# Where tokens and weight halves lie in SBUF: a 16-byte shift moved from one operand of the matmuls to the other

## The chip, the cores and the metric

The kernel runs on one core of a Trainium2 chip. The metric is the time of one execution in device microseconds: 1579.43 us is the median of three runs (1579.37 to 1579.49). One more execution was profiled; its trace is what is read below.

## The reference

One layer of an encoder on 256 tokens of width 4096, float32. What is computed:

```python
h = layer_norm(x, emb_ln_g, emb_ln_b)
p = h @ w_in                                   # 4096 x 13312: b, c, h, z of the convolution, q, k, v, z of attention
y_conv = c_b * centred_short_conv(c_c * c_h, conv_w) * silu(c_z)
y_attn = banded_window_attention(a_q, a_k, a_v, sink) * silu(a_z)   # 16 heads, 4 of keys and values, window 128
y = concatenate([y_conv, y_attn]) @ w_out      # 4096 x 4096
out = layer_norm(2 ** 0.25 * h + y, ln_g, ln_b)
```

## The kernel before

Both projections are made in a split form of float32: each operand is cut into a high half that TensorE's fp32r format holds exactly and a low half, what is left, and a product is three matmuls, high x high, high x low and low x high. The tokens are turned so that their 4096 features lie on the partitions; `xT` holds for each of 32 feature tiles 256 high and 256 low columns (1024 + 1024 bytes a partition). A slice of 128 token columns is the stationary operand of a matmul, loaded by a LDWEIGHTS of its own, and 256 columns of a weight half are the moving operand that streams past it.

The weights come from HBM in pieces of 128 x 2048 (`PIECE`) into the buffers `w0` to `w2` (and `w6` to `w8`, or free parts of `R`, where there is room). For each piece ScalarE writes the high half (`split_hi`, L201, into the tile `whi`), VectorE subtracts it for the low half (`split_lo`, L205, into `wlo`); both are rings of three tiles in the pool `wpool`. A plain piece is a step of 48 matmuls (`mm` with lines L253 to L255 for the input projection, `mm_out` with L920 to L922 for the output projection). A pair step (`mm_pair`, L277 to L279) multiplies two by two blocks with seven products in place of eight, 21 matmuls of the same shape; its stationary operands are slices of `xT` and sums of such slices that were made once: `SC` and `SC2` for the input stage (pool `psc`), `SCy` for the output stage, in the same memory as `SC`.

The order of instructions is written out by hand: a main loop over the steps issues, for step j, its matmuls, the high half for step j + 3, what is due of the attention or the convolution (transposes through `ident`, scores, exponentials, and so on), the loads of raw pieces up to seven steps ahead, and the low half for step j + 3. SP issues nearly all transfers. In the output stage `open_p2` closes the pools of the input stage and opens `p2`, with the result `R`, the parameter rows `gb` and others.

Two things of the kernel before bear on the change. The helper `shifted` makes a tile longer by 2 x `OFF` = 8 elements and hands out a view that begins 4 elements, 16 bytes, into it; `xT`, `SC` and `SC2` are made by it, `SCy`, `whi` and `wlo` are not. And small tiles named `gap` and `gap2` hold unused memory so that what follows lies where it does.

Of the kernel before, what the change touches and what calls it, by code (L numbers as in the profile page):

```python
# [8 lines left out]
F32 = mybir.dt.float32  # L9
F32R = mybir.dt.float32r  # L10
# [4 lines left out]
P = 128  # L15
D = 4096
S = 256
KT = D // P
# [9 lines left out]
PIECE = HK * P  # L28
# [4 lines left out]
W = 512  # L33
# [8 lines left out]
HT = S // 2  # L42
NP = 7
# [4 lines left out]
OP = 4  # L48
OUT_ORDERS = ["s" * 8] * 2 + ["sSsSsSsSss"] * 5 + ["", ""]
N_W = 3  # L50
OFF = 4


def units(ci):
# [45 lines left out]
def encoder_kernel(ctx: ExitStack, tc: tile.TileContext, x, emb_g, emb_b, wi, ws, conv_w, sink, wo, ln_g, ln_b, out):  # L100
# [3 lines left out]
    const = ctx.enter_context(tc.tile_pool(name="const", bufs=1))  # L104
    wpool = ctx.enter_context(tc.tile_pool(name="wpool", bufs=3))
    small = ctx.enter_context(tc.tile_pool(name="small", bufs=4))
# [9 lines left out]
    steps = IN_STEPS + OUT_STEPS  # L116
# [73 lines left out]
        return t[:, HW:] if is_pair(j) else t[:, 0:4 * HW] if steps[j][0] == "half" else t  # L190

    def half_tile(j, name):
        if j < len(steps) - 1:
            return wpool.tile([P, PIECE], F32R, name=name)
        (_, k), bs = w_bufs(j)
        user[bs[k]] = j
        return bs[k][0].tile([P, PIECE], F32R, name=bs[k][1], bufs=1)
# [20 lines left out]
    cw = const.tile([P, CONV_T, 3], F32, name="cw")  # L218
    sk = const.tile([P, HEADS], F32, name="sk")

    def shifted(pool, shape, name, **kw):

        n = math.prod(shape)
        t = pool.tile([P, n + 2 * OFF], F32R, name=name, **kw)[:, OFF:OFF + n]
        names = "abcd"[:len(shape)]
        return t.rearrange(f"p ({' '.join(names)}) -> p {' '.join(names)}", **dict(zip(names[1:], shape[1:])))

    xT = shifted(const, (KT, 2 * S), "xT")
    musd = const.tile([P, 2, 4], F32, name="musd")
    eps_t = const.tile([P, 1], F32, name="eps_t")  # L230
    nc.vector.memset(eps_t, LN_EPS)
    const.tile([P, 8], F32, name="gap")
    small.tile([P, 24], F32, name="gap2", bufs=1)


    acc = {}
# [56 lines left out]
    with tc.tile_pool(name="pro", bufs=1) as pro:  # L293
# [12 lines left out]
            sl = slice(h * PIECE // 2, (h + 1) * PIECE // 2)  # L306
            nc.sync.dma_start(out=first[1][:, sl], in_=wi[IN_PIECES.index(steps[1][1:])][:, sl])

        first = [wpool.tile([P, PIECE], F32, name=f"first{j}", tag="whi") for j in range(2)]
        x_load(0, 0, 1024, 2048, 3072, 3584, 3840, 4096)  # L310
        nc.sync.dma_start(out=g_c, in_=emb_g)
        nc.sync.dma_start(out=b_c, in_=emb_b)
# [146 lines left out]
    n_pro = 7  # L459


    ph, phs = ExitStack(), ExitStack()
    psc = ctx.enter_context(tc.tile_pool(name="psc", bufs=1))
    sc_tiles = [shifted(psc, (n, 2, 3, HT), name) for n, name in ((NP - 2, "SC"), (2, "SC2"))]
    SC = [sc_tiles[p // (NP - 2)][:, p % (NP - 2), :, :, :] for p in range(NP)]
    pw = phs.enter_context(tc.tile_pool(name="pw", bufs=1))
    extra.append((pw, "w6"))
# [98 lines left out]
    def s_add(h):  # L566
        slope = 2.0 ** (-8.0 * (h + 1) / HEADS)
        s = pa.tile([P, 2, S], F32, name="s")
        nc.vector.scalar_tensor_tensor(s, tab, slope, st_.pop(("s", h)), op0=ALU.mult, op1=ALU.add)
        m = small.tile([P, 2], F32, name="m")  # L570
        nc.vector.tensor_reduce(m, s, axis=AX.X, op=ALU.max)
        nm = small.tile([P, 2], F32, name="nm")
        nc.vector.tensor_scalar(nm, m, sk[:, h:h + 1], -1.0, op0=ALU.max, op1=ALU.mult)
        st_["sm", h] = s, nm

    def exps(h):
        s, nm = st_.pop(("sm", h))
        p = pa.tile([P, 2, S], F32, name="p", bufs=2)
        den = small.tile([P, 2], F32, name="den")
        es = small.tile([P, 2], F32, name="es")  # L580
        for b in range(2):
            nc.scalar.activation(p[:, b, :], s[:, b, :], AF.Exp, bias=nm[:, b:b + 1], accum_out=den[:, b:b + 1])
        nc.scalar.activation(es, nm, AF.Exp, bias=sk[:, h:h + 1])
        st_["p", h] = p, den, es
# [256 lines left out]
    def open_p2():  # L841
        nonlocal p2, R, st2, ms2, rows, t5, lhs5
        ph.close()
        phs.close()
        p2 = ctx.enter_context(tc.tile_pool(name="p2", bufs=1))
        R = p2.tile([P, 2, D], F32, name="R")
        st2 = [p2.tile([P, ncs, 6], F32, name=f"s2{i}") for i in range(2)]
        ms2 = p2.tile([P, 2, 4], F32, name="ms2")
        rows = p2.tile([P, 3 * W], F32R, name="rows")
        t5 = p2.tile([P, 2, 3, 32], F32, name="t5")  # L850
        nc.vector.memset(t5, 0.0)
        nc.vector.memset(t5[:, :, :, 3:5], 1.0)
        lhs5 = p2.tile([P, 2, P], F32R, name="lhs5")
# [18 lines left out]
    def res_load(n):  # L872
# [3 lines left out]
        if n < ncs - 1:  # L876
            gb = p2.tile([P, 3, w], F32, name="gb")
        if n < ncs - 2:
            xc = psc.tile([P, 2, w], F32, name="xc", tag="SC2")
        elif n == ncs - 2:  # L880
            zt.append(psc.tile([P, 8 * W], F32, name="z", tag="SC"))
            xc = zt[0][:, 6 * W:6 * W + 2 * w].rearrange("p (a b) -> p a b", a=2)
        else:
            z = zt[0]
            gb = z[:, 0:3 * w].rearrange("p (a b) -> p a b", a=3)
            xc = z[:, 3 * w:5 * w].rearrange("p (a b) -> p a b", a=2)
            g1, b1, t1 = (z[:, 5 * w + k * W:5 * w + (k + 1) * W] for k in range(3))
            first_cols.extend((g1, b1, t1, z[:, 5 * w + 3 * W:5 * w + 3 * W + P]))
            nc.sync.dma_start(out=g1, in_=bcast(ln_g, 0, W))
            nc.sync.dma_start(out=b1, in_=bcast(ln_b, 0, W))  # L890
# [109 lines left out]
    def y_sums(k):  # L1000
        nonlocal SC
        if k == 0:
            t = psc.tile([P, OP, 2, 4, HT], F32R, name="SCy", tag="SC")
            SC = [t[:, p, :, :, :] for p in range(OP)]
        x_sums(k, R[:, 0, 2 * W:4 * W])

# [126 lines left out]
```

## Time and profile before

| what | value |
|---|---|
| median of the runs | 1579.43 us |
| the profiled execution | 1580.26 us |
| its span, first to last instruction | 1578.5 us |
| granted TensorE clock | 0.999 |
| instructions | 29953, 12947 of them matmul entries on TensorE |
| moved by DMA | 316.17 MB, 200 GB/s on the mean |

In the rows below PE is TensorE's matmuls, PEld its weight loads, DVE VectorE, ACT ScalarE, POOL GpSimd, SP SyncE; L254 is line 254 of the kernel. A row that groups instructions has: line, engine, operation, tile written <- tiles read, shapes, xcount | busy us, mean ns of one | idle time of the engine before them, and what ended it. A matmul's duration in these rows is from its start until its modelled end, and successive matmuls overlap; how fast TensorE works through them is therefore seen from the distance of their starts, not from their durations. A row of one line's instructions gives the shortest, median and longest duration and, behind it, the start of the first and of the last in us; a row of the timeline begins with a start and a duration in us. A row on stretches gives the stretch, its length, the busy time of TensorE with the number of entries, the granted clock and the DMA share and rate. A row on waits says who waited <- for whom: us in all, times, longest.

### The profile page before, as it was taken

To read this page: it belongs to the slowest core of one execution; us is meant where nothing else is said; L and a number is where in the kernel's file an instruction comes from. 1 tells how busy PE (TensorE), PEld (TensorE's weight loads), DVE (VectorE), ACT (ScalarE), POOL (GpSimd) and SP (SyncE) were. 2 spreads that over 40 slices of the span, in tenths; PEclk is the share of its full clock that TensorE was granted. 3 is DMA by queue.
4 is the path that set the end of the run, shared out by engine and by line. 5 is a ranking of instruction groups with operands and counts; after the bars stand their busy time and mean duration, and the time that the engine had idled before them with its cause. 6 is when DMAs were issued, how large, how long until landed. Compare 5 with 4: busy or idle time off the path is not lost.

```text
span 1578.5 us, 29953 instructions
## 1 busy us (share of the span) xinstructions
PE 1564.9 (99%) x12947; PEld 1549.1 (98%) x12947; DVE 1331.6 (84%) x1555; ACT 780.0 (49%) x669; POOL 1.3 (0%) x7
## 2 busy tenths in 40 slices
PE   7999999999999999999999999999999999999998
PEld 4999999999999999999999999999999999999997
DVE  8669888889898898889898889888898688888866
ACT  5444546656565555544445445544455334443431
POOL 0000000000000000000000000000000000000000
PEclk9999999999999999999999999999999999999999
DMA  7545554555655555656555555556556656656563
GB/s 294 188 174 190 198 199 162 196 178 184 206 186 167 187 184 205 206 191 211 199 176 189 210 201 176 209 170 229 192 206 261 247 194 208 249 196 218 207 231 136
DMA packets 71748, 316.17 MB, mean 200 GB/s; under 512 B 8544, under 2 KB 12608, under 8 KB 50880
## 3 DMA queue, kind: packets, MB, share of 16 engines
q1 hardware_dynamic: 70608, 312.43, 57.0%
q8 instruction: 101, 1.65, 0.4%
q10 hardware_dynamic: 1008, 1.84, 0.3%
q14 instruction: 31, 0.25, 0.0%
HBM read 305.23 MB, written 8.91 MB: 199 GB/s over the span
## 4 chain that ended last, share of the span: by engine, by line
PE 98%; DVE 1%; DMA 0%; ACT 0%; issue 0%; SPq 0%; ACTq 0%
PE acc L254 15%; PE acc L253 15%; PE acc L255 15%; PE acc L920 7%; PE acc L921 7%; PE acc L922 7%; PE pacc L278 6%; PE pacc L279 6%; PE pacc L277 6%; PE acc L277 4%; PE acc L279 4%; PE acc L278 4%; PE att L492 1%; DVE st L330 0%; PE att L603 0%; PE acc L380 0%
## 5 line engine op out<-in xcount | busy, mean ns | idle before, releaser
L201 ACT ACTIVATE whi<-w 128x2048 fp32r<-128x2048 f32 (+1 forms) x354 | 620.7, 1753 | 674.6 <-PE acc L255 230.9
L205 DVE TENSOR_TENSOR wlo<-w,whi 128x2048 fp32r<-128x2048 f32 (+1 forms) x354 | 736.6, 2084 | 170.9 <-ACT whi L201 170.6
L253 PE MATMUL acc<-whi,xT 128*128 128x256 f32 x1976 | 562.7, 285 | 0.0
L254 PE MATMUL acc<-wlo,xT 128*128 128x256 f32 x1976 | 560.5, 284 | 0.0
L255 PE MATMUL acc<-whi,xT 128*128 128x256 f32 x1976 | 560.5, 284 | 0.0
L254 PEld LDWEIGHTS acc<-wlo,xT 128*128 128x128 f32 x1976 | 374.8, 190 | 0.1
L253 PEld LDWEIGHTS acc<-whi,xT 128*128 128x128 f32 x1976 | 374.9, 190 | 0.0
L255 PEld LDWEIGHTS acc<-whi,xT 128*128 128x128 f32 x1976 | 374.8, 190 | 0.0
L920 PE MATMUL acc<-whi,xT 128*128 128x256 f32 x848 | 241.4, 285 | 0.0
L922 PE MATMUL acc<-whi,xT 128*128 128x256 f32 x848 | 241.2, 284 | 0.0
L921 PE MATMUL acc<-wlo,xT 128*128 128x256 f32 x848 | 241.2, 284 | 0.0
L920 PEld LDWEIGHTS acc<-whi,xT 128*128 128x128 f32 x848 | 161.1, 190 | 0.4 <-issue 0.4
L921 PEld LDWEIGHTS acc<-wlo,xT 128*128 128x128 f32 x848 | 161.1, 190 | 0.0
L922 PEld LDWEIGHTS acc<-whi,xT 128*128 128x128 f32 x848 | 161.0, 190 | 0.0
L182 DVE TENSOR_TENSOR w<-w 128x512 f32<-128x512 f32 x179 | 122.3, 683 | 6.1 <-DMA w<-in_ws 6.1
L277 PE MATMUL acc<-whi,xT 128*128 128x256 f32 x370 | 105.0, 284 | 0.0
L279 PE MATMUL acc<-whi,xT 128*128 128x256 f32 x370 | 105.0, 284 | 0.0
L278 PE MATMUL acc<-wlo,xT 128*128 128x256 f32 x370 | 104.8, 283 | 0.0
L277 PE MATMUL pacc<-whi,xT 128*128 128x256 f32 x350 | 100.9, 288 | 0.0
L279 PE MATMUL pacc<-whi,xT 128*128 128x256 f32 x350 | 99.3, 284 | 0.0
L278 PE MATMUL pacc<-wlo,xT 128*128 128x256 f32 x350 | 99.3, 284 | 0.0
L278 PE MATMUL pacc<-wlo,SC 128*128 128x256 f32 x330 | 93.7, 284 | 0.0
(230 smaller groups left out, 2064.5 us busy)
## 6 DMA issues: line engine op xcount, KB each, us to landing
w<-in_wi SPq DMA_DIRECT2D x112, 1024.0 KB
w<-in_ws SPq DMA_DIRECT2D x202, 512.0 KB
w<-in_wo SPq DMA_DIRECT2D x41, 1024.0 KB
R<-in_wo SPq DMA_DIRECT2D x13, 1024.0 KB
x<-in_x SPq DMA_DIRECT2D x7, 512.0 KB
yl<-yd SPq DMA_DIRECT2D x7, 512.0 KB
xc<-in_x SPq DMA_DIRECT2D x14, 256.0 KB
R<-in_ws SPq DMA_DIRECT2D x6, 512.0 KB
```

Of the source, the lines that this page charges most:

```text
L182: nc.vector.tensor_tensor(s01, b22, b12.to_broadcast([P, 2, HW]), op=ALU.add)
L201: nc.scalar.activation(part(j, wh[j]), part(j, raw[j]), AF.Copy)
L205: nc.vector.tensor_tensor(part(j, wl[j]), part(j, raw[j]), part(j, wh[j]).bitcast(F32), op=ALU.subtract)
L253: nc.tensor.matmul(o, xh, hi[:, sl], start=(first and k == 0 and c == 0), stop=False)
L254: nc.tensor.matmul(o, xh, lo[:, sl], start=False, stop=False)
L255: nc.tensor.matmul(o, xl, hi[:, sl], start=False, stop=(last and k == PK - 1 and c > 0))
L277: nc.tensor.matmul(o, ah, hi[:, w, :], start=(opens and p == 0), stop=False)
L278: nc.tensor.matmul(o, ah, lo[:, w, :], start=False, stop=False)
L279: nc.tensor.matmul(o, al, hi[:, w, :], start=False, stop=(closes and last))
L920: nc.tensor.matmul(oc, yh, hi[:, sl], start=(first and c == 0), stop=False)
L921: nc.tensor.matmul(oc, yh, lo[:, sl], start=False, stop=False)
L922: nc.tensor.matmul(oc, yl, hi[:, sl], start=False, stop=(last and c + HW == w))
```

## The change

It changes where tiles lie in SBUF, and hardly anything else.

- `xT`, `SC` and `SC2` are plain tiles again; `shifted` is gone.
- `whi` tiles are 64 elements (256 bytes) longer and used from element 4 on. The ring of three `wlo` becomes three tiles of one buffer each, `wlo0` to `wlo2`, used in turn by j modulo 3, 8 elements longer and likewise used from element 4 on.
- The small tiles of the softmax (`m`, `nm`, `den`, `es`) move from the pool `small`, where each had a ring of four, into `wpool` between `wlo0`, `wlo1` and `wlo2`; `nm` and `es` have rings of three now. A loop names all tiles of `wpool` once, which sets their order in memory.
- `psc` is closed with the other pools at the start of the output stage, and `SCy`, `z` and `xc`, which lived in it, move into `p2`. `R` and what follows it lie elsewhere for that.

The places that the build gives to the operands of the matmuls (bytes within a partition; first byte of the data):

| tile | before | modulo 64, 256 | after | modulo 64, 256 |
|---|---|---|---|---|
| `xT` | 17296 | 16, 144 | 17280 | 0, 128 |
| `SC` | 157584 | 16, 144 | 158336 | 0, 128 |
| `SCy` | 157568 | 0, 128 | 158336 | 0, 128 |
| `whi`, three slots | 82944, 91136, 99328 | 0, 0 | 82928, 91376, 99824 | 48, 240 |
| `wlo`, three slots | 132096, 140288, 148480 | 0, 0 | 132848, 141296, 149744 | 48, 240 |
| raw pieces `w0` to `w2` | 107520 and on by 8192 | 0, 0 | 108256 and on by 8192 | 32, 224 |
| `ident` | 16512 | 0, 128 | 16512 | 0, 128 |
| `z`, `q`, `p`, `ug` (transposed) | 204704 (`z`) | 32, 160 | 204416 (`z`) | 0, 128 |
| `kT` (streamed), `qhl` (loaded) | 190368, 221088 | 32, 160 | 190080, 220800 | 0, 128 |

The order of instructions is the same on every engine. With numbers of lines and buffers left aside, all of them wait for the same semaphores, but for two places on TensorE. The rows are TensorE's program: line, operation, out <- moving operand, stationary operand, columns, and the semaphores that it waits for (DMAHW are those of the transfers). First the first pair step of the output stage, of before:

```order
10554 L277 MATMUL acc<-whi,xT 128x256
10555 L278 MATMUL acc<-wlo,xT 128x256
10556 L279 MATMUL acc<-whi,xT 128x256
10557 L277 MATMUL acc<-whi,SCy 128x256
10558 L278 MATMUL acc<-wlo,SCy 128x256
10559 L279 MATMUL acc<-whi,SCy 128x256
```

The same place of the changed kernel:

```order
10554 L275 MATMUL acc<-whi,xT 128x256
10555 L276 MATMUL acc<-wlo_14339,xT 128x256
10556 L277 MATMUL acc<-whi,xT 128x256
10557 L275 MATMUL acc<-whi,SCy 128x256 [waits DMAHW4_49,DMAHW5_49,DMAHW3_49,DMAHW6_49,DMAHW2_49,DMAHW7_49,DMAHW1_49,DMAHW0_49]
10558 L276 MATMUL acc<-wlo_14339,SCy 128x256
10559 L277 MATMUL acc<-whi,SCy 128x256
```

The first matmul that reads `SCy` asks for eight transfer semaphores that it did not ask for before; nothing else moved. The other place is the first transpose of the tail, of before:

```order
12697 L921 MATMUL acc<-wlo,xT 128x256
12698 L922 MATMUL acc<-whi,xT 128x256
12699 L962 MATMUL att<-ident,t_13775 96x128 [waits DMAHW4_49,DMAHW3_49,DMAHW5_49,DMAHW2_49,DMAHW6_49,DMAHW1_49,DMAHW7_49,DMAHW0_49,DVE_49]
12700 L920 MATMUL acc<-whi,xT 128x256
12701 L921 MATMUL acc<-wlo,xT 128x256
```

and of the changed kernel:

```order
12697 L922 MATMUL acc<-wlo_16939,xT 128x256
12698 L923 MATMUL acc<-whi,xT 128x256
12699 L963 MATMUL att<-ident,t_13788 96x128 [waits DVE_49]
12700 L921 MATMUL acc<-whi,xT 128x256
12701 L922 MATMUL acc<-wlo_16995,xT 128x256
```

The eight semaphores stood here and have gone from here; the wait for VectorE stays. The diff:

```diff
+GAP = 64
 ...
     def half_tile(j, name):
+        if j < len(steps) - 1 and name == "whi":
+            return wpool.tile([P, PIECE + GAP], F32R, name=name)[:, OFF:OFF + PIECE]
         if j < len(steps) - 1:
-            return wpool.tile([P, PIECE], F32R, name=name)
+            return wpool.tile([P, PIECE + 2 * OFF], F32R, name=f"{name}{j % 3}", bufs=1)[:, OFF:OFF + PIECE]
 ...
-    def shifted(pool, shape, name, **kw):
-        n = math.prod(shape)
-        t = pool.tile([P, n + 2 * OFF], F32R, name=name, **kw)[:, OFF:OFF + n]
-        names = "abcd"[:len(shape)]
-        return t.rearrange(f"p ({' '.join(names)}) -> p {' '.join(names)}", **dict(zip(names[1:], shape[1:])))
-    xT = shifted(const, (KT, 2 * S), "xT")
+    xT = const.tile([P, KT, 2 * S], F32R, name="xT")
 ...
-    small.tile([P, 24], F32, name="gap2", bufs=1)
+    for name in ("whi", "w0", "w1", "w2", "wlo0", "m", "nm", "wlo1", "den", "es", "wlo2"):
+        n = {"whi": PIECE + GAP}.get(name, PIECE + 2 * OFF if name[:3] == "wlo" else PIECE if name[0] == "w" else 2)
+        wpool.tile([P, n], F32, name=name, bufs={"whi": 3, "m": 4, "nm": 3, "den": 4, "es": 3}.get(name, 1))
 ...
-        first = [wpool.tile([P, PIECE], F32, name=f"first{j}", tag="whi") for j in range(2)]
+        first = [wpool.tile([P, PIECE + GAP], F32, name=f"first{j}", tag="whi")[:, OFF:OFF + PIECE] for j in range(2)]
 ...
-    ph, phs = ExitStack(), ExitStack()
-    psc = ctx.enter_context(tc.tile_pool(name="psc", bufs=1))
-    sc_tiles = [shifted(psc, (n, 2, 3, HT), name) for n, name in ((NP - 2, "SC"), (2, "SC2"))]
+    ph, phs, pss = ExitStack(), ExitStack(), ExitStack()
+    psc = pss.enter_context(tc.tile_pool(name="psc", bufs=1))
+    small.tile([P, 24], F32, name="gap2", bufs=1)
+    sc_tiles = [psc.tile([P, n, 2, 3, HT], F32R, name=name) for n, name in ((NP - 2, "SC"), (2, "SC2"))]
 ...
-        m = small.tile([P, 2], F32, name="m")
+        m = wpool.tile([P, 2], F32, name="m", bufs=4)
-        nm = small.tile([P, 2], F32, name="nm")
+        nm = wpool.tile([P, 2], F32, name="nm", bufs=3)
-        den = small.tile([P, 2], F32, name="den")
-        es = small.tile([P, 2], F32, name="es")
+        den = wpool.tile([P, 2], F32, name="den", bufs=4)
+        es = wpool.tile([P, 2], F32, name="es", bufs=3)
 ...
         phs.close()
+        pss.close()
         p2 = ctx.enter_context(tc.tile_pool(name="p2", bufs=1))
+        p2.tile([P, 8 * W], F32, name="SC")
 ...
-            xc = psc.tile([P, 2, w], F32, name="xc", tag="SC2")
+            xc = p2.tile([P, 2, W], F32, name="xc")[:, :, 0:w]
-            zt.append(psc.tile([P, 8 * W], F32, name="z", tag="SC"))
+            zt.append(p2.tile([P, 8 * W], F32, name="z", tag="SC"))
-            t = psc.tile([P, OP, 2, 4, HT], F32R, name="SCy", tag="SC")
+            t = p2.tile([P, OP, 2, 4, HT], F32R, name="SCy", tag="SC")
```

## The prediction

> **What bounds the kernel now.** I read the page's busy lines and its chain first, then TensorE's waits, then the starts of single matmuls, since a busy share says nothing about how far apart pipelined matmuls stand.
>
> ```profile
> span 1578.5 us, 29953 instructions
> PE 1564.9 (99%) x12947; PEld 1549.1 (98%) x12947; DVE 1331.6 (84%) x1555; ACT 780.0 (49%) x669; POOL 1.3 (0%) x7
> PEclk9999999999999999999999999999999999999999
> PE 98%; DVE 1%; DMA 0%; ACT 0%; issue 0%; SPq 0%; ACTq 0%
> ```
>
> TensorE owns 98% of the chain that ended last, at the full granted clock. Its own waits:
>
> ```profile
> PE att L393 <- DMA x<-in_x: 8.5, 1, 8.5
> PE acc L345 <- DVE x L338: 0.4, 1, 0.4
> PE att L981 <- ACT lhs L963: 0.4, 1, 0.4
> ```
>
> After the first tokens have come, nothing of weight is waited for. So an edit can move the end in two ways only: it makes TensorE wait, or it changes the spacing of its matmuls. 12,405 of the 12,947 entries are one kind, a load of 128x128 tokens (or sums of them) and a stream of 256 weight columns: 5,928 in `mm`, 3,885 in `mm_pair`, 2,592 in `mm_out`. Their spacing is read from first and last starts of one of three lines, and, for the third value, from single rows of the timeline:
>
> ```profile
> L921 PE MATMUL acc<-wlo,xT x196: 284/284/285, 1224.7 to 1294.9; 128*128 128x256 f32 x196
> ```
> ```profile
> L254 PE MATMUL acc<-wlo,xT x142: 279/280/283, 80.9 to 130.9; 128*128 128x256 f32 x142
> ```
> ```profile
> 362.75 0.28 PE L255 MATMUL acc<-whi,xT 128*128 128x256 f32 x1
> ...
> 363.80 0.28 PE L255 MATMUL acc<-whi,xT 128*128 128x256 f32 x1
> ```
>
> 70.2 us over 195 x 3 steps is 120.0 ns; 50.0 us over 141 x 3 is 118.2 ns; nine steps in 1.05 us are 116.7 ns. Each value is held for many microseconds with the same instructions and the same placement, so the streams fall into one of at least three locked rhythms, and a disturbance (a batch of transposes, a wait) picks a new one. How much of the span is at which:
>
> ```profile
> 75.00:146.00 71.00, 71.00 (x602) 1.00 0.50 179
> ...
> 240.00:660.00 420.00, 419.86 (x3532) 1.00 0.56 189
> 660.00:1202.00 542.00, 542.00 (x4525) 1.00 0.57 196
> ```
>
> The first stretch is at 118 ns. In the attention stretch (240 to 660) the rhythms alternate; if all its entries were at 118.3 it would have saved 3532 x 1.7 ns = 6 us, so I take half, 3 us. From 660 on it is nearly all 120 ns. So the faster rhythms have saved some 602 x 1.7 ns + 3 us = 4 us of the span, and 120 ns is the rule.
>
> What one of them could be at best shows at the end, where loads of the same size go with streams of 128 columns:
>
> ```profile
> 1565.89 3.12 PE pacc L1069 x28
> ```
>
> 3.12 us / 28 = 111 ns for a load and half a stream. So 120 ns holds up to 9 ns in which load and stream hinder each other, 12,405 x 9 ns = 112 us in all. That is the upper bound for anything that placement could give.
>
> The Trainium skill (TensorE: Matmul & The Clock Gate, "Step-by-step: what each phase is for", on LDWEIGHTS) says that TensorE has two independent read ports into SBUF and that loading the next weights takes no bandwidth from the running matmul; its section "Back-to-back issue gap" gives N/2.4 + 2.5 ns, an estimate of 109 ns here. By that rule placement cannot matter, the change is worth 0 and the two rivals on placement below have no chance. The rows (120, 118 and 117 ns, not 109) show a cost that the rule leaves no room for, so the trace does not agree and the rivals keep their chances.
>
> **The change, part by part.** Instruction order and semaphores first: with line and buffer numbers left aside, VectorE, ScalarE, GpSimd and SP have the same instructions with the same waits in both programs, and TensorE has the same matmuls. So the smaller rings (three buffers for `nm` and `es` instead of four), the three one-buffer tiles `wlo0` to `wlo2` in place of a ring of three, and the output stage's tiles in `p2` bring no new wait: 0.
>
> One group of waits moves: eight DMA semaphores that TensorE met in the tail, at the transpose L962, stand now before the first matmul on `SCy`. Behind it all of TensorE is queued, and every engine that waits for TensorE.
>
> ```profile
> L738 SPq DMA_DIRECT2D yl<-yd x7: 327/424/426, 1168.0 to 1213.5; - x7
> ```
> ```profile
> 1301.54 0.28 PE L279 MATMUL acc<-whi,xT 128*128 128x256 f32 x1
> 1301.66 0.28 PE L277 MATMUL acc<-whi,SCy 128*128 128x256 f32 x1
> ```
> ```profile
> 698.75 0.28 PE L279 MATMUL pacc<-whi,SC 128*128 128x256 f32 x1
> 698.87 0.60 PE L492 MATMUL att<-ident,ug 128*128 128x128 f32 x4
> ```
>
> The youngest of the transfers they ask for is the last load of `yl`, issued at 1213.5, 88 us before. A like group, nine semaphores before the transposes at 698.87, left the spacing at 0.12 us. So it costs 0 as long as those 88 us stand; without them TensorE would stand still until the load lands.
>
> Now the shift itself on ScalarE and VectorE. Before, tokens lay 16 bytes up and the halves did not; the change turns this round. Equal shapes with and without the shift stand side by side:
>
> ```profile
> L205 DVE TENSOR_TENSOR wlo<-w,whi 128x1024 fp32r<-128x1024 f32 x23 | 28.1, 1222 | 10.0 <-ACT whi L201 9.9
> L386 DVE TENSOR_TENSOR xT<-hT,xT 128x1024 fp32r<-128x1024 f32 x8 | 9.8, 1226 | 0.3
> ```
> ```profile
> L201 ACT ACTIVATE whi<-w 128x1024 fp32r<-128x1024 f32 x23 | 24.4, 1060 | 82.2 <-PE acc L255 78.4 <-issue 3.8
> L748 ACT ACTIVATE xT<-yl 128x1024 fp32r<-128x1024 f32 x7 | 7.3, 1044 | 0.0
> ```
>
> 1222 against 1226 ns and 1060 against 1044 ns: the shift costs neither engine more than 0.3% of an instruction. Even if it cost 10%, the halves are ready ahead of need, since ScalarE waits for TensorE to give their buffers back:
>
> ```profile
> ACT whi L201 <- PE acc L255: 230.9, 100, 4.1
> ```
> ```profile
> L205 DVE TENSOR_TENSOR wlo<-w,whi 128x2048 fp32r<-128x2048 f32 (+1 forms) x354 | 736.6, 2084 | 170.9 <-ACT whi L201 170.6
> ```
>
> These edits go in at 0, hidden behind TensorE; without that cover, 0.3% of 736.6 us is 2 us.
>
> What is left is the spacing. From the placement of the tiles (the table in the section on the change): tokens less weights was 144 modulo 256 bytes and is 144 again; the sums in `SC` too. Both sides moved down by 16 bytes. The 256 bytes more between the slots of `whi`, and between those of `wlo`, change the distance only from bit 8 up, and the rows above show no trace of such bits: in the 196 starts at 120 ns the token tile steps through multiples of 512 bytes while the weights step by 1024. If the rhythm hangs on the distance, nothing changes there: 12,405 x 0.
>
> Only one kind of step has another distance now than before. `SCy` lay at 128 modulo 256 against weights at 0; now it is 144 from them like all else. A pair step has 21 matmuls; one on `SC`, then one on `SCy`, first start to next step's first start:
>
> ```profile
> 1039.89 0.28 PE L277 MATMUL pacc<-whi,xT 128*128 128x256 f32 x1
> ...
> 1042.41 0.28 PE L253 MATMUL acc<-whi,xT 128*128 128x256 f32 x1
> ```
> ```profile
> 1398.30 0.28 PE L277 MATMUL pacc<-whi,xT 128*128 128x256 f32 x1
> ...
> 1400.80 0.28 PE L920 MATMUL acc<-whi,xT 128*128 128x256 f32 x1
> ```
>
> 2.52 us with the shift, 2.50 us (each to 0.01) where 12 of the 21 loads are unshifted. There are 20 such steps: the change adds 20 x 0.02 = 0.4 us.
>
> Bounds for the spacing, which the trace of the old placement cannot give: below, 111 ns each (112 us less); above, if a stream that starts 48 bytes into a block of 64 pays for one block more in 17, 1/16 of at most 111 ns, 6.9 ns or 86 us more. I take 0 because the distance is kept and both ends need the rhythm to depend on absolute places.
>
> **The sum.** The profiled execution took 1580.26 us for its span of 1578.5 us (1.8 us lie around it); it is 0.8 us over the median of the runs, 1579.43. Its sum changes by 0 + 0 + 0.4 us to 1580.7, and the median to 1579.8 us.
>
> **The rivals.**
> - *Faster: the token side decides by its own place.* Before, each load of 512 bytes began 16 bytes into a block of 64; now it begins on one. For it speaks the step on `SCy`: 0.02 us over its 12 unshifted loads is 1.7 ns a load, just the distance from 120 to 118.3. Over 12,405 matmuls that is 21 us less, of which 4 us are had already: 17 us, 1563 us. Against it: in those steps the distance changed as well, so they don't tell which of the two it was. One rhythm further, 116.7, gives 12,405 x 3.3 - 4 = 37 us, 1542 us; both hold from the first step on.
> - *Slower: the stream's own place decides.* Streams of weights began on a block of 64 bytes and now begin 48 bytes into one; if that costs a notch of the same 1.7 ns, 120 becomes 121.7: 21 us more and the 4 us lost, 1604 us. It decides from any cost that isn't hidden in the 9 ns of slack between 111 and 120. Against it: nothing in the trace starts there; the nearest, keys streamed from 32 bytes into a block, take 282 ns each, no more than the 284 of the weights:
>
> ```profile
> L563 PE MATMUL att<-kT,qhl 128*128 128x256 f32 x32 | 9.0, 282 | 0.0
> ```
>
> - *Slower by a little: every stretch locks at 120.* The transposes of `z`, `q`, `p` and `ug` change their distance to the identity (32 to 0 modulo 64 bytes), and they are what picks the next rhythm. If all stretches then fall to 120, the 4 us are lost: 1584 us. If the long stretch after 660 falls to 118.3 instead, 4525 x 1.7 = 8 us are won: 1572 us.
>
> **How the numbers follow.** About 0.2%, 3 us, is what a measurement of this kernel can tell from no change. Forecast (spacing as before, within 3 us): 0.47. Token place decides: 0.22, and the long stretch at 118.3: 0.10, together 0.32 for faster with a rest for larger gains. Weights' place decides: 0.09; all at 120: 0.12, together 0.21 for slower. The likeliest gives 1579.8 us, its own range 1577 to 1583. The range for 8 in 10 reaches to the first faster rhythm below and over the loss of all fast stretches, with half a notch of the weights' cost, above: 1563 to 1588 us.
>
> **What would show it.** Right: first and last start of L254 and L921 in the new profile give 120.0 ns in the output stage and 118 ns after the first stage, and the step on `SCy` takes 2.52 us. Token place: the output stage at 118.3 ns or less. Weights' place: over 120.5 ns anywhere. Transposes: the same three values, in other stretches. The moved waits: a gap over 0.15 us before the first matmul on `SCy`. For VectorE and ScalarE, means more than 1% from these would break the claim that the shift costs them nothing:
>
> ```profile
> L205 DVE TENSOR_TENSOR wlo<-w,whi 128x2048 fp32r<-128x2048 f32 x152 | 347.8, 2288 | 107.9 <-ACT whi L201 107.8
> ```
> ```profile
> L201 ACT ACTIVATE whi<-w 128x2048 fp32r<-128x2048 f32 x152 | 291.5, 1918 | 278.6 <-PE acc L255 97.4 <-PE acc L922 80.0 <-issue 57.2
> ```

## The result, and the profile after

The changed kernel takes 1524.81 us (median; 1524.3 to 1524.95) where the kernel before takes 1579.40 us: 54.6 us less, a ratio of 0.9654 (95% interval 0.9637 to 0.9671). The prediction was 1579.8 us, no change, with 1563 to 1588 us as its range. It was wrong.

The page of the changed kernel: busy times, then the engines' shares of the chain that ended last.

```profile
span 1523.2 us, 29953 instructions
PE 1501.5 (99%) x12947; PEld 1478.8 (97%) x12947; DVE 1329.8 (87%) x1555; ACT 783.4 (51%) x669; POOL 1.3 (0%) x7
PE 79%; DVE 15%; ACT 3%; issue 2%; DMA 1%; SPq 0%; ACTq 0%; DVEq 0%
```

The work is the same, TensorE is still called 99% busy, but VectorE now owns 15% of the chain (1% before). What the busy share hides is in the starts. `mm`, `mm_pair` and `mm_out` are now at lines 251 to 253, 275 to 277 and 921 to 923; of one line each, in the output stage and in the second stage:

```profile
L922 PE MATMUL acc<-wlo,xT x198: 275/275/275, 1184.9 to 1251.9; 128*128 128x256 f32 x198
L252 PE MATMUL acc<-wlo,xT x148: 275/275/275, 77.8 to 127.8; 128*128 128x256 f32 x148
```

67.0 us over 197 x 3 steps is 113.4 ns, where it was 120.0; 50.0 us over 147 x 3 is 113.4 ns, where it was 118.2. This is a fourth rhythm, held nearly everywhere, 2 ns above the 111 ns that the prediction took as the floor. Over all 12,405 matmuls, leaving out gaps of 126 ns and more, the mean of the steps from one start to the next fell from 119.65 to 113.75 ns: 73 us. Only 55 us of it arrived. Of the other 18 us, 13 lie in gaps of 126 ns and more between these matmuls (what such gaps have beyond a usual step rose from 4 to 17 us), and 5 in the stretches of other matmuls, transposes and scores among them (71.8 us before, 76.7 now). The stretch of the last input chunks, before and then after (PE, PEld, DVE, ACT, POOL busy, clock, DMA share, GB/s):

```profile
660.00:1202.00 542.00, 542.00 (x4525) 542.00 (x4524) 478.64 (x520) 268.50 (x179) 0.00 (x0) 1.00 0.57 196
```
```profile
641.00:1163.00 522.00, 518.78 (x4519) 514.67 (x4518) 477.93 (x518) 269.82 (x179) 0.00 (x0) 1.00 0.58 203
```

VectorE has the same 478 us of work, in 522 us instead of 542, and TensorE has holes that it had not before. What it waits for (us in all, times, longest), matmuls and then loads:

```profile
PE acc L252 <- DVE wlo L208: 3.2, 6, 0.7
PE att L602 <- DVE s L568: 2.2, 4, 0.6
PE acc L922 <- DVE wlo L208: 1.0, 2, 0.7
```
```profile
PEld acc L252 <- DVE wlo L208: 8.2, 23, 0.9
```

So there are two questions: what made the streams 6 ns closer, and what it would take to get the 18 us that seem to go to waits for VectorE.

### The profile page after: what moved, and what is told of

It is laid out like the page before. It is cut to its first block, busy times and chain, and to the rows that moved or that the text cites. A ratio compares the mean times of both kernels' runs of the same rounds, so it can differ in the third digit from the quotient of the medians.

```text
span 1523.2 us, 29953 instructions
## 1 busy us (share of the span) xinstructions
PE 1501.5 (99%) x12947; PEld 1478.8 (97%) x12947; DVE 1329.8 (87%) x1555; ACT 783.4 (51%) x669; POOL 1.3 (0%) x7
## 4 chain that ended last, share of the span: by engine, by line
PE 79%; DVE 15%; ACT 3%; issue 2%; DMA 1%; SPq 0%; ACTq 0%; DVEq 0%
PE acc L252 13%; PE acc L253 12%; PE acc L251 12%; DVE wlo L208 9%; PE acc L922 6%; PE acc L923 6%; PE acc L921 6%; PE pacc L277 4%; PE pacc L276 4%; PE pacc L275 4%; PE acc L277 3%; PE acc L275 3%; PE acc L276 3%; ACT whi L204 3%; DVE w L183 2%
## 5 line engine op out<-in xcount | busy, mean ns | idle before, releaser
L252 PE MATMUL acc<-wlo,xT 128*128 128x256 f32 x1976 | 547.7, 277 | 3.7 <-DVE wlo L208 3.2
L251 PE MATMUL acc<-whi,xT 128*128 128x256 f32 x1976 | 547.0, 277 | 0.0
L253 PE MATMUL acc<-whi,xT 128*128 128x256 f32 x1976 | 544.5, 276 | 0.0
L252 PEld LDWEIGHTS acc<-wlo,xT 128*128 128x128 f32 x1976 | 371.1, 188 | 8.7 <-DVE wlo L208 8.2
L251 PEld LDWEIGHTS acc<-whi,xT 128*128 128x128 f32 x1976 | 371.1, 188 | 0.0
L253 PEld LDWEIGHTS acc<-whi,xT 128*128 128x128 f32 x1976 | 371.0, 188 | 0.0
L922 PE MATMUL acc<-wlo,xT 128*128 128x256 f32 x848 | 233.5, 275 | 1.0 <-DVE wlo L208 1.0
L921 PE MATMUL acc<-whi,xT 128*128 128x256 f32 x848 | 233.6, 275 | 0.0
L923 PE MATMUL acc<-whi,xT 128*128 128x256 f32 x848 | 233.3, 275 | 0.0
L922 PEld LDWEIGHTS acc<-wlo,xT 128*128 128x128 f32 x848 | 159.2, 188 | 1.4 <-DVE wlo L208 1.4
L921 PEld LDWEIGHTS acc<-whi,xT 128*128 128x128 f32 x848 | 159.2, 188 | 0.4 <-issue 0.4
L923 PEld LDWEIGHTS acc<-whi,xT 128*128 128x128 f32 x848 | 159.2, 188 | 0.0
L275 PE MATMUL acc<-whi,xT 128*128 128x256 f32 x370 | 102.1, 276 | 0.0
L276 PE MATMUL acc<-wlo,xT 128*128 128x256 f32 x370 | 102.1, 276 | 0.0
L277 PE MATMUL acc<-whi,xT 128*128 128x256 f32 x370 | 102.0, 276 | 0.0
L275 PE MATMUL pacc<-whi,xT 128*128 128x256 f32 x350 | 98.1, 280 | 0.0
L277 PE MATMUL pacc<-whi,xT 128*128 128x256 f32 x350 | 96.4, 276 | 0.0
L277 PE MATMUL pacc<-whi,SC 128*128 128x256 f32 x330 | 90.9, 275 | 0.0
```

The costliest lines, as they stand in the source:

```text
L251: nc.tensor.matmul(o, xh, hi[:, sl], start=(first and k == 0 and c == 0), stop=False)
L252: nc.tensor.matmul(o, xh, lo[:, sl], start=False, stop=False)
L253: nc.tensor.matmul(o, xl, hi[:, sl], start=False, stop=(last and k == PK - 1 and c > 0))
L275: nc.tensor.matmul(o, ah, hi[:, w, :], start=(opens and p == 0), stop=False)
L276: nc.tensor.matmul(o, ah, lo[:, w, :], start=False, stop=False)
L277: nc.tensor.matmul(o, al, hi[:, w, :], start=False, stop=(closes and last))
```

## The experiments

**Which operand's place decides?** Four kernels: the tokens' shift alone taken away (all else as before), and the changed kernel with the halves 16 bytes higher, 16 bytes lower, and with the tokens up again.

```
before, tokens at 64:    - t = pool.tile([P, n + 2 * OFF], ...)[:, OFF:OFF + n]
                         + t = pool.tile([P, n + 2 * OFF], ...)[:, 0:n]
change, weights at 64:   - [:, OFF:OFF + PIECE]      + [:, 8:8 + PIECE]     (three places)
change, weights at 32:   - [:, OFF:OFF + PIECE]      + [:, 0:0 + PIECE]     (three places)
change, tokens up again: - xT = const.tile(...)      + xT = shifted(const, (KT, 2 * S), "xT")
                         - const.tile([P, 8], F32, name="gap")    (SC, SC2 shifted as well)
```

> The kernel before with one edit: tokens and sums of x start at their tiles' first byte, 16 bytes lower, on a block of 64 bytes; every tile stays where it was, the weights' halves too, with the old pitch of 8192 bytes. Theory T (the token side's own place decides): the matmuls fall from 120.0 to 113.3 ns apart and the run takes about 1525 us. Theory W (the halves must lie 48 bytes into a block of 64): 120 ns or more, 1579 us or more. Theory P (the 256 bytes between the slots of the halves, so bits from 8 up): 120 ns, about 1580 us. Theory S (the output stage's pool, the small tiles between the slots): 120 ns, about 1580 us.

> The changed kernel with the weights' halves 16 bytes higher inside their tiles, so that they start on a block of 64 bytes as the tokens do; all tiles in their new places. T: 113.3 ns, about 1525 us. W: 120 ns, about 1580 us. P and S: 113.3 ns, about 1525 us.

> The changed kernel with the weights' halves at their tiles' first byte, 32 bytes into a block of 64, as the raw weights are. T: 113.3 ns, about 1525 us. W: 118 to 120 ns, 1565 to 1580 us. P and S: 113.3 ns, about 1525 us.

> The changed kernel with tokens and sums of x shifted up again by 16 bytes (the sums of the last two pieces by 48), the weights' halves left in their new places, 48 bytes into a block of 64, with the new pitch. T: 120 ns, about 1580 us. W, P and S: 113.3 ns, about 1525 us.

Ratios to the kernel before: 0.994 (0.9923 to 0.9957; 1569.2 us), 0.9938 (0.9918 to 0.9958; 1568.8 us), 1.0032 (1.002 to 1.0043; 1584.1 us) and 1.0023 (1.0014 to 1.0032; 1582.3 us). No theory had this. The output stage of the first, then of the last:

```profile
L921 PE MATMUL acc<-wlo,xT x198: 279/281/285, 1214.7 to 1284.9; 128*128 128x256 f32 x198
```
```profile
L928 PE MATMUL acc<-wlo,xT x198: 282/283/284, 1225.8 to 1296.7; 128*128 128x256 f32 x198
```

70.2 us / 591 = 118.8 ns and 70.9 / 591 = 120.0 ns. Any one of the two sides moved by itself loses most or all of the gain. One thing is settled: the first two kernels differ in pools, slots and small tiles and agree in the two operands' places, and they agree in time within 0.5 us. So the places are all that counts; the rest of the change is worth nothing.

**A table without the encoder.** Loads and streams alone, in the kernel's order of triples, with the other engines idle; and with it, in the whole kernel, a shorter gap between the slots of the first halves.

```
- GAP = 64
+ GAP = 16      (slots of whi at 240, 48, 112 modulo 256, slots of wlo at 176)
```

> No part of the encoder: only loads of 128x128 and streams of 256 columns (some of 128, 64 and 512), in the order of the kernel's triples, 48 or 72 for each pair of starts of the two operands, the other engines idle; the output is zeros. Names: t, then the token side's place in a block of 64 bytes (a 0, e 16, i 32, m 48), then that of the weights (a 0, b 4, ... e 16, i 32, m 48, p 60), then the length (m 256, h 128, q 64, f 512). Theory PP (the two places modulo 64 decide together, with nobody else): 256 columns take 113.3 ns at 0 and 48, 118.7 at 0 and 0, 120 at 0 and 32, at 16 and 0 and at 16 and 48; places 64, 128 and 192 bytes further change nothing. Theory R (the other engines' reads and writes of the same memory set the rhythm): one value, near 109 to 113 ns, at all places. Theory Q (it hangs on bits 6 and 7 too): other values 64, 128 or 192 bytes further.

> The changed kernel with 64 bytes instead of 256 between the slots of the first halves: all streams still start 48 bytes into a block of 64, but modulo 256 the slots lie at 240, 48 and 112, and the second halves at 176. PP: 113.3 ns, 1525 us. Q (the place modulo 256 counts): only the first slot keeps it, that is 2 of 9 matmuls; the others at 118.7 to 120 ns, 1559 to 1569 us.

For 256 columns the table holds no single value: leaving out its first entry, with which the clock came up, it runs from 113.3 to 123.3 ns, so neither ScalarE, VectorE nor transfers are needed for the effect. At 0 and 48, where theory PP expects 113.3 ns, it has 118.3 and 118.4. Its few entries 64 to 240 bytes further gave the lead: 113.3 to 113.7 ns stood at only four of them, two with the tokens 64 and two with them 144 bytes ahead of the weights modulo 256, wherever both lay. The short gap gave 0.983 (0.9814 to 0.9847; 1552.3 us), between the two forecasts, with a mean step of 117.3 ns, though all its streams start 48 bytes into a block of 64: two places modulo 64 do not decide alone, and the distance modulo 256, which is 144 in one of its slots only, counts.

A second table by distance was to confirm it:

> No part of the encoder: loads of 128x128 and streams of 256 columns alone, 60 for each pair of places, the output zeros; each pair three times, both operands 0, 64 and 128 bytes up, forwards, backwards, forwards. Names: x, the token side's place in a block of 64 bytes (a 0, b 16, c 32, d 48), d and the distance tokens less weights modulo 256 in steps of 16 bytes (a 0, b 16, e 64, i 128, j 144, k 160). Theory D (token's place in the block and the distance modulo 256 decide): the three turns agree within a notch; xa_de (0, 64) and xa_dj (0, 144) 113.3 to 113.6 ns, xa_di 118.7, xb_dj 120.0, xb_dk 120.0. Theory M (absolute places of both within 256 bytes): the turns differ, above all xa_de and xa_dj, which would keep 113 ns in only one of them.

It came to 116.7 to 120.0 ns everywhere and showed nothing of 113 ns, at first sight against theory D. In it the second halves lay 128 bytes off the first halves modulo 256 (the tile had become 8576 bytes long, 33.5 x 256). But it does speak against theory M: in its third turn, with both operands 128 bytes higher than in the first, 63 of the 64 pairs took the same time within 0.02 ns and the last within 0.2. (The turn backwards differs from them by up to 2.2 ns, as the turns of the next table do at equal places; so what ran before has a share too.) The third table has both halves at one place:

```
- WL = 2048 + 96
+ WL = 2048 + 128      (34 x 256 bytes; and a start of its own for the second halves)
```

> As the table by distance, loads and streams of 256 columns alone, but with second halves that lie, modulo 256 bytes, where the first halves lie (in the table by distance they lay 128 bytes off, which was not meant, and all places came to 117 to 120 ns). Names: x, place of the tokens modulo 64 (a 0, b 16, c 32, d 48), then two letters, the distance tokens less weights modulo 256 in 16-byte steps for the first halves and for the second (a 0, e 64, i 128, j 144, m 192). Theory D2 (the tokens' place modulo 32 or 64 with the distances of both halves): xa_dee and xa_djj 113.3 to 113.6, xa_dii 118.7, xb_djj 120.0; with the first halves at e or j and the second halves elsewhere a value of its own for each pair of letters, near 117.7 for e with m. Theory H (history: which rhythm is found is a matter of what ran before): xa_dee and xa_djj differ between their turns and after 1 to 16 short streams; at e both 113.3 and 118, as the run with distance 64 showed stretches of both; at j always 113.3 to 113.6.

Four of its 128 runs of 48 matmuls, first and last start of each (timeline of the third table; the letters after x are the token's place, those after d the distance, for first and second halves):

```profile
76.97 0.28 PE L66 MATMUL xa_djj<-whi,xT 128*128 128x256 f32 x1
...
82.29 0.28 PE L66 MATMUL xa_djj<-whi,xT 128*128 128x256 f32 x1
82.41 0.28 PE L66 MATMUL xa_dii<-whi,xT 128*128 128x256 f32 x1
...
87.97 0.28 PE L66 MATMUL xa_dii<-whi,xT 128*128 128x256 f32 x1
...
173.12 0.28 PE L66 MATMUL xb_djj<-whi,xT 128*128 128x256 f32 x1
...
178.75 0.28 PE L66 MATMUL xb_djj<-whi,xT 128*128 128x256 f32 x1
...
201.68 0.28 PE L66 MATMUL xb_dee<-whi,xT 128*128 128x256 f32 x1
...
207.03 0.28 PE L66 MATMUL xb_dee<-whi,xT 128*128 128x256 f32 x1
```

Over 47 steps each: 113.2 ns at distance 144 with the tokens at 0 (the changed kernel's places), 118.3 at distance 128, 119.8 at distance 144 with the tokens at 16 (those of the kernel before), 113.8 at distance 64 with the tokens at 16. The whole table, from all starts but the first six of each run, two turns:

```
distance   tokens at 0 and 32   tokens at 16 and 48 (modulo 64)
   0       119.9 - 120.0        118.3 - 118.4
  16       117.0 - 117.2        118.3
  32       118.3 - 118.4        119.9 - 120.0
  48       119.2                117.8 - 123.2
  64       113.3                113.3 - 113.6
  80       119.2 - 119.4        118.7 - 118.9
  96       117.3 - 117.4        116.7 - 117.8
 112       116.7 - 118.7        120.1 - 120.2
 128       118.7 - 119.9        120.0
 144       113.3 - 114.0        120.0
 160       120.0                120.0
 176       119.9                118.0
 192       117.8                118.3
 208       118.3 - 118.4        116.6 - 116.7
 224       116.6 - 117.8        118.3
 240       116.6 - 118.6        117.3 - 120.0
```

With first halves at 144, second halves at 144 gave 113.3 ns and the other 15 distances 117.7 to 120.0; with first halves at 64, all 16 gave 115.7 to 118.9 (both at 64, this time, 117.8). After 1 to 16 short streams, distance 144 came back to 113.3 ns 16 times of 16 and distance 64 13 times, with 117.8 ns for the whole of the other three. So both theories on record hold a part: the tokens' place modulo 32 and both distances decide, and at 64 there are two rhythms. Whether what ran before or chance picks one of them, a single execution cannot tell.

**Does the law hold in the whole kernel?** Distance 64, reached from the kernel before by two edits and nothing of the change's pools; and distance 64 in the changed kernel with the tokens 16 bytes up as before.

```
before, distance 64:            - [:, OFF:OFF + n]                          + [:, 0:n]
                                - const.tile([P, 8], F32, name="gap")       + const.tile([P, 24], ...)
                                - small.tile([P, 24], F32, name="gap2", ..) + small.tile([P, 8], ...)
change, tokens up, distance 64: - xT = const.tile(...)                      + xT = shifted(...)
                                - const.tile([P, 8], F32, name="gap")       + const.tile([P, 24], ...)
                                - small.tile([P, 24], F32, name="gap2", ..)   (SC, SC2 shifted as well)
```

> The kernel before with two edits: tokens and sums of x at their tiles' first byte (as in the first experiment, 1569 us alone), and 64 bytes moved from the second padding to the first, so that all weights' halves lie 64 bytes higher; pitch, pools and small tiles as before. All operands start on a block of 64 bytes, tokens less weights is 64 modulo 256. D: 113.3 ns and 1523 to 1526 us, as the whole change. M or a theory by which weights must lie 48 bytes into a block: 118.7 ns, 1569 us. If pools, pitch or small tiles of the change have a share of the gain: in between.

> The changed kernel with tokens and sums of x 16 bytes up again, as they were before the change, and all weights' halves moved so that tokens less weights is 64 modulo 256 (for the sums of the last two pieces 96, for the sums of the output stage 48). Theory D2 (the table: at distance 64 the tokens' own place does not count): mostly 113.3 ns, some stretches at 117.8, 1526 to 1540 us. Theory T32 (tokens must start on a multiple of 32 bytes, as the change has it): 118 ns or more, 1565 to 1582 us.

0.9721 (0.9706 to 0.9737; 1536.7 us) and 0.9678 (0.9664 to 0.9692; 1527.5 us). The first is slower than the 1523 to 1526 us of theory D. It has both rhythms of distance 64, for tens of microseconds each; its second stage and its output stage:

```profile
L253 PE MATMUL acc<-whi,xT x148: 281/281/281, 77.8 to 129.7; 128*128 128x256 f32 x148
L921 PE MATMUL acc<-wlo,xT x160: 276/276/276, 1199.9 to 1254.0; 128*128 128x256 f32 x160
```

51.9 us / 441 = 117.7 ns and 54.1 / 477 = 113.4 ns. Its four executions spread from 1532.8 to 1539.0 us. In the profiled one, the fastest, the stretches at 117.7 ns cost 12,405 x (114.62 - 113.75) = 11 us against the change, and shorter gaps give 3 of them back. The second kernel keeps the tokens where they were, and is 0.2% behind the change: the tokens' place on a multiple of 32 is not needed, once the distance is 64. The kernels of these experiments whose slots have one distance, with the mean of their steps under 126 ns in the profiled execution and the median time:

```
kernel                          tokens mod 32  distance  table          in the kernel   time
before                               16          144     120.0          119.65 ns       1579.4 us
the change                            0          144     113.3 - 114.0  113.75          1524.8
before, tokens at 64                  0          128     118.7 - 119.9  118.70          1569.2
change, weights at 64                 0          128     118.7 - 119.9  118.68          1568.8
change, weights at 32                 0          160     120.0          119.87          1584.1
change, tokens up again              16          160     120.0          119.84          1582.3
before, distance 64                   0           64     113.3, 117.8   114.62          1536.7
change, tokens up, distance 64       16           64     113.3 - 113.6  114.06          1527.5
```

Why these distances and no others is not shown by any run.

**Where 18 us of the gain went.** Two ways to take work from VectorE. First, two of the three additions that a pair's weights need go to GpSimd, which is idle:

```
- nc.vector.tensor_tensor(r(6), r(5), r(1), op=ALU.add)     + nc.gpsimd.tensor_tensor(...)
- nc.vector.tensor_tensor(r(7), r(6), r(3), op=ALU.add)     + nc.gpsimd.tensor_tensor(...)
```

> The changed kernel with two of the three additions that a pair's weights need (two of 128x256 each, 2 x 185 instructions, 0.43 us each) on GpSimd in place of VectorE: 157 us less for VectorE. Theory V (some 15 us of the matmuls' gain are given back since TensorE waits for VectorE's second halves): up to 15 us faster than the change, 1510 to 1525 us, with fewer gaps before the middle matmul of the triple. Rival G (GpSimd takes over a microsecond for each, and ScalarE's first half waits for it): slower than the change, 1530 us or more, ScalarE's wait for the sums over 135 us in the stretch from 641 to 1163.

0.9976 (0.9965 to 0.9986; 1576.7 us): nearly all of the gain gone, the rival. GpSimd's groups, and then what ScalarE waits for from 661 to 1205 us:

```profile
L184 POOL TENSOR_TENSOR w<-w 128x256 f32<-128x256 f32 x179 | 306.7, 1713 | 771.6 <-DVE w L183 501.6 <-issue 124.9 <-ACT whi L204 95.1
L185 POOL TENSOR_TENSOR w<-w 128x256 f32<-128x256 f32 x179 | 170.9, 955 | 14.0
```
```profile
ACT whi L204 <- POOL w L185: 232.5, 63, 7.8
```

Such an addition takes 425 ns on VectorE in the changed kernel:

```profile
L185 DVE TENSOR_TENSOR w<-w 128x256 f32<-128x256 f32 x179 | 76.1, 425 | 6.2
```

The two of GpSimd, 955 and 1713 ns (its spans are rough), stand ahead of the first half that ScalarE makes and the second half that VectorE makes of it. The Trainium skill (GPSIMD Engine Reference, "4.1 Engine selection") calls GpSimd some 2 times slower for elementwise work with two inputs; here it was 2.2 and 4.0 times. Second, the same two additions left out; a copy on ScalarE stands in their place, so this kernel does not compute the layer:

```
- nc.vector.tensor_tensor(r(6), r(5), r(1), op=ALU.add)     + nc.scalar.activation(both, copied, AF.Copy)
- nc.vector.tensor_tensor(r(7), r(6), r(3), op=ALU.add)
```

> The changed kernel with the last two of a pair's additions left out: one copy of 128x512 on ScalarE stands in their place, so the sums of those two blocks are wrong and their products with them; 157 us less for VectorE, some 100 us more for ScalarE, which is half idle. Theory V (waits for VectorE's second halves give back some 15 us): 1508 to 1516 us, the streams of over 126 ns back from 17 to some 5 us. Rival N (those long gaps are not VectorE's): 1524 us.

0.9567 (0.9551 to 0.9583; 1507.3 us). TensorE's waits for second halves are gone and it owns the chain again:

```profile
PE 97%; ACT 2%; issue 1%; DMA 0%; DVE 0%; SPq 0%; ACTq 0%
```

Span against span, 1505.6 against 1523.2 us, 17.6 us were lost to VectorE's lateness, and 73 less 55 is 18. The starts agree: what the gaps of 126 ns and more have beyond a usual step falls back from 17 to 5 us, and the stretches of other matmuls from 76.7 to 71.9 us.

The work need not go, though. Sorted by their place in a chunk (from the starts of all matmuls), the changed kernel's gaps of 126 ns and more sit at two whole pieces: 7.5 us in 23 chunks at the piece in sixth place, behind a pair, the half step and a pair, and 4.0 us at the piece in ninth place, behind two pairs. In the kernel before it was 0.4 and 0.9 us there. (The expectation for the next kernels, below, puts these sums at the chunk's first piece and at the pair behind the half step; the starts do not bear that out.) In one chunk, from the start of the pair in third place to that of the piece in sixth:

```profile
832.78 0.28 PE L275 MATMUL pacc<-whi,xT 128*128 128x256 f32 x1
833.03 1.71 ACT L204 ACTIVATE whi<-w 128x1792 fp32r<-128x1792 f32 x1 [1.31 <-DVE wlo L208]
834.77 2.03 DVE L208 TENSOR_TENSOR wlo<-w,whi 128x1792 fp32r<-128x1792 f32 x1 [1.80 <-ACT whi L204]
836.71 0.68 DVE L183 TENSOR_TENSOR w<-w 128x512 f32<-128x512 f32 x1
838.23 2.29 DVE L208 TENSOR_TENSOR wlo<-w,whi 128x2048 fp32r<-128x2048 f32 x1
840.26 0.28 PE L251 MATMUL acc<-whi,xT 128*128 128x256 f32 x1
840.57 0.19 PEld L252 LDWEIGHTS acc<-wlo,xT 128*128 128x128 f32 x1 [0.23 <-DVE wlo L208]
```

With the end of the pair in second place, at 832.78, one of the three buffers of first halves is free. ScalarE fills it for the pair in fifth place (its row names VectorE, which ended at 832.97; TensorE's last matmul on that buffer ended at 832.95, and in the kernel before this start follows TensorE by the same 0.25 us). VectorE makes that pair's second half, the three additions for the pair in seventh place (the first is shown), and the second half of the piece in sixth place. This chain takes 7.74 us (median of 20 chunks). TensorE has 66 matmuls to do in that time, 7.48 us at 113.4 ns, and waits. At 120 ns it took 7.92 us, and the same chain, 7.73 us there, stayed hidden. In some chunks VectorE's additions hold the first half back longer, and the wait grows. Two kernels with another order of the steps:

```
- ORDERS = {..., NP: "sSShSsSSsSSs"}      + "sSSsSSsSShSs" (late)      + "sSSsSShSsSSs" (mid)
```

> The changed kernel with another order of the steps of a full chunk: the half step goes from the fourth place to the tenth, a whole piece takes its place (s S S s S S s S h S s in place of s S S h S s S S s S S s, s a piece, S a pair, h the half step, the rest as it follows). Theory V (the middle matmuls' long gaps, half of them at the chunk's first piece and a quarter at the pair behind the half step, come from VectorE's backlog): the 4 us at the fifth place go, 1519 to 1523 us. Rival: the backlog comes back at the pair behind the half step in its new place or at the next chunk's first piece: 1524 us or more.

> As the one with the half step late, with the half step at the seventh place (s S S s S S h S s S S s shortened by none). V: 1519 to 1523 us. Rival: 1524 us or more.

0.9575 (0.9561 to 0.9589; 1510.9 us) and 0.9617 (0.9603 to 0.9631; 1517.6 us). Both beat the change, and both come out below the 1519 to 1523 us of theory V, whose forecast rested on the wrong places. With the half step late, its run of pair, half step and pair stands before the chunk's last piece, and behind that comes another piece, not a pair: the three additions drop out of the chain, which takes 6.99 us against TensorE's 7.60. The sums of the long gaps fall to 0.5 us there, and to 1.1 and 1.0 us at the pieces in fourth and seventh place; over the whole kernel from 17 to 9 us, and the stretches of other matmuls from 76.7 to 71.3 us. With the half step in the middle, the run stands before the piece in ninth place, a pair follows, and 4.3 us of gaps are found at that piece. Of the late one, what the loads of second halves wait for (8.2 us in the change), and the chain that ended last:

```profile
PEld acc L252 <- DVE wlo L208: 1.4, 5, 0.6
PE 92%; DVE 5%; DMA 1%; issue 1%; ACT 1%; SPq 0%; ACTq 0%; DVEq 0%
```

VectorE does the same 1331 us of work in it. It is the fastest kernel here that computes the whole layer, 4.3% under the kernel before.

## Why the prediction was wrong

- *TensorE is the bound, and an edit moves the end by a wait or by the spacing.* Right, and both happened: the spacing gave 73 us, new waits took 18.
- *The floor of 111 ns, 112 us in all.* It held: no kernel and no table came under 113.3 ns for long with streams of 256 columns.
- *Order, pools, small tiles and the eight moved waits cost 0.* Right. Kernels with and without them agree within 0.5 us, and the first matmul on `SCy` starts 0.11 us after the one before it:

```profile
1258.11 0.28 PE L277 MATMUL acc<-whi,xT 128*128 128x256 f32 x1
1258.22 0.28 PE L275 MATMUL acc<-whi,SCy 128*128 128x256 f32 x1
```

- *The shift costs ScalarE and VectorE nothing.* Right for the instructions, 2288 ns as before and 1928 for 1918:

```profile
L208 DVE TENSOR_TENSOR wlo<-w,whi 128x2048 fp32r<-128x2048 f32 x152 | 347.8, 2288 | 80.5 <-ACT whi L204 80.3
L204 ACT ACTIVATE whi<-w 128x2048 fp32r<-128x2048 f32 x152 | 293.0, 1928 | 226.1 <-PE acc L253 75.8 <-PE acc L923 72.3 <-issue 44.2
```

  Their idle time shrank (107.9 to 80.5 us for this form). The claim that they are hidden behind TensorE held for a TensorE at 120 ns (7.73 us of work against 7.92) and no longer at 113 (7.74 against 7.48); the prediction did not ask what a faster bound would uncover.
- *"If the rhythm hangs on the distance, nothing changes there: 12,405 x 0."* This step failed. The part on the bits was right: multiples of 256 bytes in the distance change nothing. But at a distance of 144 the tokens' own place modulo 32 decides between 120.0 and 113.3 ns, and the change moved just that, from 16 to 0. The prediction took "same distance" for "same rhythm", though it had written down that tokens and weights both moved by 16 bytes, and no row of the old placement could have a step with another token place at the same distance. The term was 12,405 x 5.9 ns = 73 us less, not 0.
- *The steps on `SCy`, 0.4 us more.* Wrong in sign: each of the 20 steps takes 2.38 us now (2.50 before), 2.5 us less together, and nearly all steps on `SC` take 2.38 us as well.

```profile
1357.51 0.28 PE L275 MATMUL pacc<-whi,xT 128*128 128x256 f32 x1
...
1359.88 0.28 PE L921 MATMUL acc<-whi,xT 128*128 128x256 f32 x1
```

- *The rival on the tokens' place* had the sign, and its condition was met only because the distance was kept too. It read its price, 1.7 ns (1.3 ns over all steps on `SC` and `SCy`), off steps on `SCy` with tokens at 0 and a distance of 128, where the table has 118.7 ns and more: that was the price of the first experiment (1.0 ns, 10 us), not of the change. Its own objection, that in those steps the distance moves as well, was the missing half of the law.
- *The rival on the weights' place* is out: streams that start 48 bytes into a block of 64 are among the fastest.
- *The rival on the transposes* is out: of the first two kernels of the experiments one has `z`, `q`, `p` and `ug` at their old places and one at the new, and they agree within 0.5 us.
- *The skill's rule against it.* The Trainium skill (SBUF — State Buffer, "A bandwidth-pool intuition that's wrong (but worth ruling out)") gives TensorE a second, independent read port for its loads. With all other engines idle, load and stream still stood 113.3 to 123 ns apart by the distance of their two start addresses, so the runs do not agree that the two reads are independent; where they meet, no run shows. The 109 ns beside that rule in the prediction were no fair test of it: the Trainium skill (TensorE: Matmul & The Clock Gate, "Back-to-back issue gap") gives N/2.4 + 2.5 for an isolated matmul, and says that it under-counts at small N, for want of the loads. Here streams of 128 columns with their loads took 111.6 ns, where the formula gives an estimate of 56.

## What to carry to other kernels

In a stream of short loads and short streams, the spacing can hang on the distance of the two operands' addresses modulo 256 bytes and on where one of them starts. Read the spacing from first and last starts, and try a few distances (for 128-column loads with 256-column streams of 4-byte elements it was 64, or 144 with the loaded operand on a multiple of 32, and both halves of the streamed operand at the same distance). A shift of one operand alone changes the distance, and a shift of both by the same 16 bytes still changed the spacing here; a shift of both by 128 bytes did not. When a trace holds only one placement, an argument that "the relation is kept" is a guess about the other placements. And before writing that an engine is hidden behind the bound, ask at what speed of the bound it comes out: here at 113 ns, where the order of steps, not the amount of work, was worth another 14 us.

## What the hardware showed that was not expected

- With nothing else running, the spacing of a 128x128 load with a 256-column stream took values from 113.3 to 123 ns, by the two start addresses and to a lesser part by what ran before. With 128-column streams there was nothing of it, 111.6 to 111.8 ns at 16 places of the first table; with 512 columns it took 226.7 to 233.4 ns.
- At one and the same placement (distance 64) two rhythms are stable, 113.3 and 117.8 ns, for 10 us in the table and for tens of microseconds in the kernel; at distance 144 with the tokens on a multiple of 32 the stream found back to 113.3 ns within 15 matmuls.
- In the first table's stretch with streams of 64 columns the granted clock fell to half, and they took 213 ns each, more than those of 128:

```profile
PEclk9999999999999999999999999999999955559999
```

- GpSimd took 1713 ns for an addition of 128x256 that took VectorE 425 ns, and 955 ns for the next one of the same shape (GpSimd's spans are rough).
